# A gradient kernel: the first store of each trio on a second queue, ahead of the end of the last load

## Chip, core, metric

One core of one Trainium2 chip. The metric is the device time of the kernel in microseconds, median of several executions.

## The reference

```python
x = np.random.randn(8192, 8192).astype(np.float32)
def reference(x):
    return np.gradient(x, axis=1)
```

Along each row, an inner element becomes half the difference of its right and left neighbours; the two row ends become plain differences. Input and output are 268.4 MB each.

## The kernel before

32 tiles, each 128 partitions x two rows of 8192 floats (8.39 MB), go through three slots in SBUF. For each tile: a load, a tiny subtraction on GpSimd that puts the row ends aside (POOL in the profile), one pass on VectorE (DVE) that halves the differences, in place and shifted by 64 columns, a tiny copy that places the row ends, and a store. All transfers go through the sync engine's queue, in runs of three loads and three stores.

```python
R, NB, SH = 2, 3, 64                       # rows a tile, slots, shift
def load(i):
    b = slots[i % NB]
    ins = nc.sync.dma_start(out=b[:, SH : SH + W], in_=x_sets[i])
    loads.append(chain(i, ins, *([stores[i - NB]] if i >= NB else [])))   # waits for the slot's store

for i in range(NB): load(i)
for i in range(nsets):
    ins = nc.gpsimd.tensor_sub(out=ends[:, i], ...)           # row ends put aside
    at = [chain(i, ins, loads[i])]
    last = i == nsets - 1
    nr = 1 if last else R                                     # the last tile goes in two rows
    for r in range(0, R, nr):
        ins = nc.vector._custom_dve(...)                      # 0.5 * (right - left)
        halved = chain(i, ins, *at)
        placer = nc.gpsimd if i % 5 in (1, 3) and not last else nc.vector
        ins = placer.tensor_copy(...)                         # row ends placed
        placed = chain(i, ins, halved)
        ins = nc.sync.dma_start(out=out_sets[i, ...], in_=b[...])
        stores[i] = chain(i, ins, placed)
        at = [halved]
    if i % NB == NB - 1:                                      # three loads after three stores
        for k in range(i + 1, min(i + 1 + NB, nsets)): load(k)
```

## Time and profile before

| | before |
|---|---|
| time, median of the first 3 executions | 1248.08 us (1247.47 to 1248.88) |
| span of the profiled execution | 1245.0 us |
| moved | 536.88 MB, 431 GB/s over the span |
| VectorE busy | 45% |
| share of the 16 DMA engines' span taken by packets | 99.8% |

A page of the profile has, among others, the busy time of each engine, a row of 40 slices of the span (the busy share of the DMA engines in tenths, and GB/s), the DMA queues with their packets, and groups of instructions (line, engine, operation, shapes, count, busy us, mean ns, idle time before them and its cause). Two groups of before; after the first bar stand the busy time (us) and the mean duration (ns), after the second the idle time (us) and what ended it:

```profile
L81 DVE CUSTOM_DVE_ANT_0 slot<-slot 128x16382 f32<-128x16382 f32 (+1 forms) x33 | 551.3, 16706 | 667.9 <-POOL ends L70 667.9
L92 DVE COPY slot<-ends 128x4 f32<-128x4 f32 (+1 forms) x21 | 3.6, 172 | 0.7
```

VectorE has 667.9 us of idle time: nothing that it is spared can shorten the kernel by itself.

Below the page lie the trace's records of single DMA packets (start, duration, bytes, queue). No view prints them, so where I use them I give sums. They name neither the engine nor the direction: packets are joined end to start into 16 chains, one for each engine, and the order in which the transfers were issued tells loads from stores. Counts of matched packets are therefore good to a few per cent only. The landings on single engines are the trace's semaphore updates, 16 for each transfer; no view prints these either. A "long packet" is one of 65,536 bytes that took over 2.47 us instead of 2.418. The "packet excess" is the time of all packets above 2.418 us (1.21 for halves), from 5 us into the span on, divided by 16: what a mean engine lost. Before: 3.10 us.

### The profile page before, as it was taken

How to read it: one execution, taken by the hardware profiler on the slowest of the kernel's cores; microseconds unless marked ns; L12 is line 12 of the kernel's file. 1: busy time of each engine (PE TensorE's matmuls, PEld its weight loads, DVE VectorE, ACT ScalarE, POOL GpSimd, SP SyncE). 2: the span in 40 equal slices, each digit the busy share in tenths (PEclk: the TensorE clock that was granted, in tenths of full speed). 3: DMA queues.
4: the chain of work that ended last, by engine and by line, in shares of the span. 5: the costliest groups of instructions: out<-in, count | busy, mean ns of one | idle time of the engine just before them, and what ended most of it. 6: DMA issues, size and time to landing. Idle time of an engine off the chain costs nothing.

```text
span 1245.0 us, 241 instructions
## 1 busy us (share of the span) xinstructions
DVE 554.8 (45%) x54; POOL 8.8 (1%) x48
## 2 busy tenths in 40 slices
DVE  2850483079009603850582079009603840591083
POOL 0000000000000000000000000000000000000000
DMA  9999999999999999999999999999999999999999
GB/s 404 438 436 419 425 438 438 438 438 438 434 427 421 436 438 438 436 438 432 432 419 438 436 438 432 436 434 432 423 436 436 436 438 436 430 427 430 436 411 404
DMA packets 9361, 536.88 MB, mean 431 GB/s; under 512 B 1040, under 2 KB 1040, under 8 KB 1040
## 3 DMA queue, kind: packets, MB, share of 16 engines
q1 hardware_dynamic: 9360, 536.88, 99.8%
q14 instruction: 1, 0.01, 0.0%
HBM read 268.44 MB, written 268.44 MB: 431 GB/s over the span
## 4 chain that ended last, share of the span: by engine, by line
another core or an unknown queue 74%; DVE 18%; DMA 3%; issue 2%; POOL 1%; SPq 0%; POOLq 0%
DVE slot L81 18%; DMA slot<-in_x_dram 3%; POOL ends L70 0%; POOL slot L92 0%; SPq L60 0%; DVE slot L92 0%; POOLq L127 0%
## 5 line engine op out<-in xcount | busy, mean ns | idle before, releaser
L81 DVE CUSTOM_DVE_ANT_0 slot<-slot 128x16382 f32<-128x16382 f32 (+1 forms) x33 | 551.3, 16706 | 667.9 <-POOL ends L70 667.9
L70 POOL TENSOR_TENSOR ends<-slot 128x4 f32<-128x4 f32 x32 | 6.3, 198 | 988.8 <-DMA slot<-in_x_dram 988.8
L92 DVE COPY slot<-ends 128x4 f32<-128x4 f32 (+1 forms) x21 | 3.6, 172 | 0.7
L92 POOL COPY slot<-ends 128x4 f32<-128x4 f32 x12 | 2.3, 190 | 207.9 <-DVE slot L81 207.9
L116 POOL MEMSET const-bfloat16-1.0<- 128x1 bf16 x1 | 0.1, 102 | 0.0
L116 POOL MEMSET const-uint8-127<- 128x1 uint8 x1 | 0.1, 102 | 0.0
L116 POOL MEMSET const-float32-0.0<- 128x1 f32 x1 | 0.1, 99 | 0.2 <-issue 0.2
L116 POOL MEMSET const-float32-1.0<- 128x1 f32 x1 | 0.1, 99 | 0.0
## 6 DMA issues: line engine op xcount, KB each, us to landing
out_dram<-slot SPq DMA_DIRECT2D x2, 4096.0 KB, 20.2
slot<-in_x_dram SPq DMA_DIRECT2D x32, 58.0
out_dram<-slot SPq DMA_DIRECT2D x31, 40.3
```

Source lines behind the costliest of these rows:

```text
L70: ins = nc.gpsimd.tensor_sub(out=ends[:, i, :, :], in0=xin[:, :, 1 : m : m - 2], in1=xin[:, :, 0 : m - 1 : m - 2],)
L81: ins = nc.vector._custom_dve(dve_ops.TENSOR_TENSOR_REDUCE_SUB_MAX, out=b[:, c0:c1], in0=b[:, SH + c0 + 1 : SH + c1 + 1], in1=b[:, SH + c0 ...
L92: ins = placer.tensor_copy(out=res[:, :, 0 : m : m - 1], in_=ends[:, i, r : r + nr, :])
L116: nc = _bacc.Bacc("TRN2", target_bir_lowering=False, num_devices=1)
```

## The change

The intent: don't let the first store of a trio wait in the queue behind the last load. It goes on the ACT (ScalarE) queue and is let go when the first row of the middle tile is halved, so the engines have stores at hand before the loads are through. The middle tile's pass is cut in two rows to give that moment; ScalarE and GpSimd place the row ends. At the end, tile 29 counts as a "first": its store is held back behind loads 30 and 31.

```diff
+    next_loads = {i: range(i + 1, i + 1 + NB) for i in range(NB - 1, n3 - NB, NB)}
+    next_loads[n3 - 2] = range(n3, nsets)              # n3 = 30: loads 30, 31 after tile 28
+    firsts = [*range(0, n3, NB), n3 - 1]
     ...
-            nr = 1 if last else R
-            ...
-                placer = nc.gpsimd if i % 5 in (1, 3) and not last else nc.vector
-            ...
-            if i % NB == NB - 1:
-                for k in range(i + 1, min(i + 1 + NB, nsets)):
-                    load(k)
+            if i - 1 in firsts and i not in firsts or last:
+                at = halve(i, 0, 1, at)
+                if last:
+                    store(nc.sync, i, 0, 1, place(nc.vector, i, 0, 1, at))
+                else:
+                    store(nc.scalar, i - 1, 0, R, placed, at)      # the first store, gated
+                at = halve(i, 1, 1, at)
+            else:
+                at = halve(i, 0, R, at)
+            if last:
+                store(nc.sync, i, 1, 1, place(nc.vector, i, 1, 1, at))
+            else:
+                placed = place(nc.gpsimd if i % 4 == 1 else nc.scalar, i, 0, R, at)
+                if i not in firsts:
+                    store(nc.sync, i, 0, R, placed)
+            for k in next_loads.get(i, ()):
+                load(k)
```

(The helpers `store`, `halve`, `place` and `put_aside` hold the same calls as before.)

More of the change, by code (lines that the diff above doesn't have):

```diff
@@ L4 @@
 import concourse.tile as tile
-from concourse import bass_utils, dve_ops
+from concourse import bass_utils, dve_ops, mybir
 from concourse._compat import with_exitstack
@@ L41 @@
     ends = pool.tile([P, nsets, R, 2], f32, name="ends", tag="ends")
+    landed = mybir.DependencyInfo(mybir.DependencyClass.Sync, mybir.DependencyReason.DATA)
     loads, stores = [], [None] * nsets
@@ L61, in load, with store, put_aside, halve @@
         loads.append(chain(i, ins, *([stores[i - NB]] if i >= NB else [])))
+    n3 = (nsets - 2) // NB * NB
+    assert nsets - 2 == n3
+    next_loads = {i: range(i + 1, i + 1 + NB) for i in range(NB - 1, n3 - NB, NB)}
+    next_loads[n3 - 2] = range(n3, nsets)
+    def store(queue, i, r, nr, *needed):
+        ins = queue.dma_start(
+            out=out_sets[i, :, r * m : (r + nr) * m], in_=slots[i % NB][:, r * m : (r + nr) * m]
+        )
+        stores[i] = chain(i, ins, needed[0])
+        for o in needed[1:]:
+            tc.add_manual_dep(ins.ins, o.ins.name, landed, reason="before the end of the last load")
+    def put_aside(i):
+        xin = slots[i % NB][:, SH : SH + W].rearrange("p (t m) -> p t m", m=m)
+        ins = nc.gpsimd.tensor_sub(
+            out=ends[:, i, :, :],
+            in0=xin[:, :, 1 : m : m - 2],
+            in1=xin[:, :, 0 : m - 1 : m - 2],
+        )
+        return chain(i, ins, loads[i])
+    def halve(i, r, nr, at):
+        b = slots[i % NB]
+        c0, c1 = r * m + 1, (r + nr) * m - 1
+        ins = nc.vector._custom_dve(
+            dve_ops.TENSOR_TENSOR_REDUCE_SUB_MAX,
+            out=b[:, c0:c1],
+            in0=b[:, SH + c0 + 1 : SH + c1 + 1],
+            in1=b[:, SH + c0 - 1 : SH + c1 - 1],
+            s0=0.0,
+            s1=0.5,
+        )
+        return chain(i, ins, at)
+    def place(engine, i, r, nr, at):
+        res = slots[i % NB][:, r * m : (r + nr) * m].rearrange("p (t m) -> p t m", m=m)
+        to, of = res[:, :, 0 : m : m - 1], ends[:, i, r : r + nr, :]
+        ins = nc.scalar.copy(out=to, in_=of) if engine is nc.scalar else engine.tensor_copy(out=to, in_=of)
+        return chain(i, ins, at)
+    firsts = [*range(0, n3, NB), n3 - 1]
     with tc.manual_schedule():
@@ L66 @@
         for i in range(nsets):
-            b = slots[i % NB]
-            xin = b[:, SH : SH + W].rearrange("p (t m) -> p t m", m=m)
-            ins = nc.gpsimd.tensor_sub(
-                out=ends[:, i, :, :],
-                in0=xin[:, :, 1 : m : m - 2],
-                in1=xin[:, :, 0 : m - 1 : m - 2],
-            )
-            at = [chain(i, ins, loads[i])]
-            last = i == nsets - 1
-            nr = 1 if last else R
-            for r in range(0, R, nr):
-                c0, c1 = r * m + 1, (r + nr) * m - 1
-                ins = nc.vector._custom_dve(
-                    dve_ops.TENSOR_TENSOR_REDUCE_SUB_MAX,
-                    out=b[:, c0:c1],
-                    in0=b[:, SH + c0 + 1 : SH + c1 + 1],
-                    in1=b[:, SH + c0 - 1 : SH + c1 - 1],
-                    s0=0.0,
-                    s1=0.5,
-                )
-                halved = chain(i, ins, *at)
-                res = b[:, r * m : (r + nr) * m].rearrange("p (t m) -> p t m", m=m)
-                placer = nc.gpsimd if i % 5 in (1, 3) and not last else nc.vector
-                ins = placer.tensor_copy(out=res[:, :, 0 : m : m - 1], in_=ends[:, i, r : r + nr, :])
-                placed = chain(i, ins, halved)
-                ins = nc.sync.dma_start(
-                    out=out_sets[i, :, r * m : (r + nr) * m], in_=b[:, r * m : (r + nr) * m]
-                )
-                stores[i] = chain(i, ins, placed)
-                at = [halved]
@@ L99 @@
-            if i % NB == NB - 1:
-                for k in range(i + 1, min(i + 1 + NB, nsets)):
-                    load(k)
+            at = put_aside(i)
+            last = i == nsets - 1
+            if i - 1 in firsts and i not in firsts or last:
[7 more added lines that the diff above has]
+                at = halve(i, 0, R, at)
```

## The prediction

> **What bounds the kernel now.** I read the page first, then who waited for whom, then the GpSimd and queue rows in order of time, and last the trace's records of single DMA packets. The page:
>
> ```profile
> span 1245.0 us, 241 instructions
> DVE 554.8 (45%) x54; POOL 8.8 (1%) x48
> ...
> DMA  9999999999999999999999999999999999999999
> ...
> q1 hardware_dynamic: 9360, 536.88, 99.8%
> ...
> HBM read 268.44 MB, written 268.44 MB: 431 GB/s over the span
> ```
>
> The reader is to see that one queue keeps the 16 DMA engines busy 99.8% of the span, while VectorE, the only busy engine, works 45% of it. The array is read once and written once, so the bytes can't shrink. In the packet records nearly every packet of 65,536 bytes takes 2.418 us on its engine: 16 x 65,536 / 2.418 us = 433.7 GB/s. 536.88 MB at that rate are 1238.0 us. The first packet starts at 1.75 us and the last bytes are confirmed at 1244.1 us, so of the 1245.0 us of the profile 1238 are plain transfer, 1.75 start, about 1 end, and only some 4 us are spread over the middle. Everything that the change can win lies in those 4 us.
>
> Where do they lie? Each GpSimd subtraction starts 0.07 us after a load has landed, so its rows in order of time are a clock of the landings (start, duration, instruction, and in brackets the idle time before it). Two trios of loads and the last two loads:
>
> ```profile
> 22.70 0.20 POOL L70 TENSOR_TENSOR ends<-slot 128x4 f32<-128x4 f32 x1 [22.26 <-DMA slot<-in_x_dram]
> 42.04 0.20 POOL L70 TENSOR_TENSOR ends<-slot 128x4 f32<-128x4 f32 x1 [19.14 <-DMA slot<-in_x_dram]
> ...
> 62.45 0.20 POOL L70 TENSOR_TENSOR ends<-slot 128x4 f32<-128x4 f32 x1 [2.71 <-DMA slot<-in_x_dram]
> ...
> 721.14 0.20 POOL L70 TENSOR_TENSOR ends<-slot 128x4 f32<-128x4 f32 x1 [77.06 <-DMA slot<-in_x_dram]
> ...
> 740.49 0.20 POOL L70 TENSOR_TENSOR ends<-slot 128x4 f32<-128x4 f32 x1 [1.64 <-DMA slot<-in_x_dram]
> 760.50 0.20 POOL L70 TENSOR_TENSOR ends<-slot 128x4 f32<-128x4 f32 x1 [19.81 <-DMA slot<-in_x_dram]
> ...
> 1186.19 0.20 POOL L70 TENSOR_TENSOR ends<-slot 128x4 f32<-128x4 f32 x1 [77.05 <-DMA slot<-in_x_dram]
> 1205.53 0.20 POOL L70 TENSOR_TENSOR ends<-slot 128x4 f32<-128x4 f32 x1 [19.14 <-DMA slot<-in_x_dram]
> ```
>
> A tile of 8.39 MB takes 8 x 2.418 = 19.34 us. The second load of a trio lands 19.34 us after the first (42.04 - 22.70), but the third comes 20.41 us after the second in the first trio and 20.01 us in the one at 760. Over all ten trios the third load is late by 1.06, 0.01, 0.01, 0.04, 0.50, 0.61, 0.66, 0.17, 0.27 and 0.00 us: 3.3 us in all. The stretches from a third load to the next first load (three stores and a load) are four tiles long, 77.25 to 77.40 us against 77.38, and give 0.6 us of it back. So the slowest engine loses about 2.8 us in the kernel, all at the switch from loads to stores; the other switch, from stores to loads, is free. The packet records say the same: it is the last load packet of each engine before the first store that is long (3.2 to 3.5 us at 58 us, 2.6 to 3.2 at 639), averaged over the engines 0.24 us a switch.
>
> The last view is the queue's own waits and the end of the timeline:
>
> ```profile
> SPq L94 <- DVE slot L92: 525.7, 21, 55.9
> SPq L60 <- DMA out_dram<-slot: 373.2, 29, 19.2
> ```
> ```profile
> 1203.68 0.17 DVE L92 COPY slot<-ends 128x4 f32<-128x4 f32 x1
> 1203.88 19.93 SPq L94 DMA_DIRECT2D out_dram<-slot  x3
> ```
>
> These long waits are of the issuing sequencer, with up to three transfers queued ahead, and cost nothing: a store issued at 157.57 us runs only when the third load is through at 178.5. The one exception is the end. The store of tile 30 is issued at 1203.88 us, when the load of tile 31 ends on the 16 engines between 1202.9 and 1205.5 us. The early engines idle about 1.5 us on average, but the slowest has no gap: its next store lands at 1224.8, one tile after 1205.46. That hole evens out the engines' skew rather than costing the end.
>
> **What the Trainium skill says.** "DMA: Bandwidth & Descriptors", section "Where 436 GB/s comes from", puts the ceiling of the 16 ports at 435.2 GB/s; the trace agrees, 433.7 in the packets. The same page, "Issuing engines are not separate DMA queues", says that DMAs of the scalar and sync engines end up on the same 16 engines and interleave: no bandwidth is to be had from the second queue. Its section "Queues, rings and completion order" says that each engine takes turns between the queue rows that have work, a packet at a time; the trace of before uses one queue and can't show it, and my estimate below takes equal turns. "ScalarE: Activation LUTs", section "What ACT_TABLE_LOAD costs", measures 1283 ns for the load that ScalarE will need once; there is no ScalarE work in this trace to compare.
>
> **The change part by part.**
>
> 1. *Placing row ends.* 19 whole-tile VectorE copies of 172 ns (3.3 us) and some GpSimd ones go, and ScalarE does most of the placing. VectorE idles 667.9 us, so this is worth 0 on the path. A ScalarE copy of four elements might take 0.3 us instead of 0.17; it delays a store's issue by 0.1 us, with many us of queue ahead. The table load comes while the first load runs (22 us). 0 us.
>
> 2. *Row-wise middle tile.* One pass of 17.22 us becomes two of 8.69 and 8.60 as in the last tile of before: +0.1 us on an engine at 45%. 0 us.
>
> 3. *First store on the other queue.* Take the round whose loads land at 139.8, 159.1 and 178.5. The first row of the middle tile is done at 159.4 + 8.7 = 168.1 us. The store goes out then and starts about 1 us later (the first load was issued at 0.74 and moved at 1.75). Now the third load has 9.3 us left, and with equal turns ends at 169.2 + 18.6 = 187.8 instead of 178.5. The first store has by then done half; it shares the engines with the middle store and ends at 187.8 + 2 x 10.0 = 208. The third tile's pass ends at 188 + 17.4 = 205.5, and its store is queued at 206. Loads and two stores together fill the engines until 120.5 + 5 x 19.34 = 217.2 us, so the third store is there 11 us before it is needed. The next load waits for the first store (208), long before the queue reaches it at 236.5; the two after it wait for stores at 217 and 236.5, in time too. No new hole: the bytes still set the time, 0 us from scheduling.
>
> 4. *What the overlap does to the switch.* This is the disputed part. At best the engine has packets of both kinds in hand and the long last load packet goes away: -2.8 us on the slowest engine. At worst each load packet followed by a store packet pays the 0.24 us: 9.3 / 2.418, nearly 4 switches per engine and round instead of 1, so 3 x 0.24 x 10 = +7 us.
>
> 5. *The end.* Tile 29 is held back: loads 30 and 31 are now queued after the store of 28, and the store of 29 runs beside load 31. It fills the hole at 1203, and the last tile still goes out in two halves with nothing after it. The 1.5 us is the mean engine's, none of it the slowest's; I count 0, or some tenths if skew no longer builds up.
>
> Sum: -2.8 at best, +7 at worst. I weigh the good case somewhat higher, because the switch within one ordered queue is what seems to hold the last load packet up: about -1 us.
>
> **The rivals.** (a) *The switch vanishes*: 1248.1 - 2.8 = 1245.3 us. For it: two queues let an engine fetch from both sides; the loss stands only where a load meets a store in one queue. (b) *Mixing costs*: every alternation pays, 1248.1 + 7 = 1255 us. For it: the loss is seen on each engine just where the two directions meet. Against it: in two of ten rounds it was 0.01 us or less with the same meeting. (c) *Unequal turns*: if the sync queue were served first, the first store would starve behind two others, the next load would wait for it, and about 2 us per round would be empty: +20 us, 1268. If the other queue came first, the third load would land 19.3 us late, at 198, and its store be issued at 216, just when the engines run dry at 217: about 1 us a round, 1258. (d) *Nothing changes* since the switch to mixed stores only moves: 1248.
>
> **Range and chances.** (a) or a part of it has about half of the weight, (d) a quarter, (b) a fifth, (c) a twentieth. That gives 1247.0 us with 1244.0 to 1255.0 for 8 in 10. A floor stands at about 1244, since the transfer alone takes 1238.0 us, so over 2% faster (1223) is all but excluded: 0.01. Over 2% slower (1273) needs (c) or worse: 0.02. Within 2%: 0.97.
>
> **What would show it.** Right: DMA still 9 in all 40 slices; two queues, the new one with 10 to 11 stores (92 MB of 536.88); third loads landing 27 to 29 us after the second instead of 19.4 to 20.4; packet times of 2.418 us (or twice that where two overlap) with no long load packets at the switch; ScalarE under 10 us busy. If (b), dips in the GB/s row at every overlap and longer periods between the first loads of trios than 116.1 to 116.7 us. If (c), the sync queue's waits on stores end after the engines ran dry, and a slice falls below 9. The prediction is wrong if the packet rate itself differs when reads and writes of the HBM are mixed for about 19 us in each round, in either direction.

## The result, and the profile after

| | before | after |
|---|---|---|
| median | 1248.21 us (6 runs) | 1248.91 us (6 runs) |
| range | 1247.16 to 1248.94 | 1248.20 to 1249.84 |
| packet excess, profiled execution | 3.10 us | 5.63 us |
| last store landed on the first / the last of the 16 engines | 1243.9 / 1244.1 us | 1244.2 / 1246.8 us |

The ratio is 1.0006, with a 95% interval of 0.9993 to 1.0019. A ratio is the mean time of one kernel's fast runs over that of the other's fast runs of the same rounds, so not quite the ratio of the medians. Executions over 1.5% slower than the fastest of the same kernel are left out of the means. Unaltered in a later set of runs (b0 below) the changed kernel stood at 1.0017 (1.0005 to 1.0029). The profiled execution of after happened to be the slowest of its six.

The page of after, the rows that answer to those shown of before:

```profile
span 1247.8 us, 258 instructions
DVE 553.3 (44%) x46; ACT 5.8 (0%) x24; POOL 8.1 (1%) x44
...
DMA  9999999999999999999999999999999999999998
...
q1 hardware_dynamic: 7776, 444.60, 82.7%
q10 hardware_dynamic: 1584, 92.28, 17.1%
...
L110 ACT COPY slot<-ends 128x4 f32<-128x4 f32 x23 | 4.5, 197 | 1180.3 <-DVE slot L97 1180.3
...
L110 ACT ACT_TABLE_LOAD x1 | 1.3, 1283 | 0.7 <-PEq L151 0.7
```

The second queue, q10, carries 11 stores (92.28 MB); the two queues add up to the same 99.8%. ScalarE is busy 5.8 us. The engines are as full as before, so the scheduling left no hole; only the last slice has an 8.

Who waited on the sync queue, after:

```profile
SPq L76 <- ACT slot L110: 616.5, 15, 56.3
SPq L65 <- DMA out_dram<-slot: 326.6, 29, 33.8
```

As before these are waits of the sequencer with transfers queued ahead of it. They cost nothing as long as the DMA row stays full.

The second round of after in order of time (start, duration, engine, instruction; "x2" merges two issues, the second one 0.34 us before the end of the stretch):

```profile
140.10 0.20 POOL L86 TENSOR_TENSOR ends<-slot 128x4 f32<-128x4 f32 x1 [69.91 <-DMA slot<-in_x_dram]
...
159.45 0.20 POOL L86 TENSOR_TENSOR ends<-slot 128x4 f32<-128x4 f32 x1 [19.16 <-DMA slot<-in_x_dram]
...
168.45 0.34 ACTq L76 DMA_DIRECT2D out_dram<-slot  x1
...
177.35 27.60 SPq L76 DMA_DIRECT2D out_dram<-slot  x2
186.87 0.20 POOL L86 TENSOR_TENSOR ends<-slot 128x4 f32<-128x4 f32 x1 [27.23 <-DMA slot<-in_x_dram]
...
210.97 26.94 SPq L65 DMA_DIRECT2D slot<-in_x_dram  x3
```

And the same three landings in before:

```profile
139.84 0.20 POOL L70 TENSOR_TENSOR ends<-slot 128x4 f32<-128x4 f32 x1 [77.19 <-DMA slot<-in_x_dram]
159.18 0.20 POOL L70 TENSOR_TENSOR ends<-slot 128x4 f32<-128x4 f32 x1 [1.64 <-DMA slot<-in_x_dram]
178.54 0.20 POOL L70 TENSOR_TENSOR ends<-slot 128x4 f32<-128x4 f32 x1 [19.16 <-DMA slot<-in_x_dram]
```

The POOL rows are the landings. The third load lands 27.4 us after the second (19.4 in before), because from 173 us on it shares the engines with the first store. The first store is issued at 168.45 us and has landed by 210.95, where the next load is issued. The third store is issued at 177.35 + 27.60 - 0.34 = 204.6 us; the middle one landed on the slowest engine at 218.2. So the queue had some 12 us in hand.

Inside the overlap the packet records alternate: after one packet of q10 on an engine comes one of q1, then one of q10, each 2.418 to 2.427 us long. That is the equal turn that was assumed. (Once a round, where the sync queue passes from the third load to the middle store, q10 has two turns in a row.) The long packets haven't gone away. They stand once per round at the place where the first store comes in: at 53.2 us, where the packet of the third load just ahead of the first store packet took 3.4 to 3.9 us on all 16 engines, and so on near 170, 288, 404, 520 us. 182 of them are load packets directly ahead of a q10 packet. An engine goes from a load packet to a store packet about three times in an overlap, and of the three it is nearly always the first that is long. Before, they stood at 58.2 us and at the ends of the third loads.

### The profile page after: what moved, and what is told of

It is laid out like the page before. It is cut to its first block, busy times and chain, and to the rows that moved or that the text cites. A ratio compares the mean times of both kernels' runs of the same rounds, so it can differ in the third digit from the quotient of the medians.

```text
span 1247.8 us, 258 instructions
## 1 busy us (share of the span) xinstructions
DVE 553.3 (44%) x46; ACT 5.8 (0%) x24; POOL 8.1 (1%) x44
## 3 DMA queue, kind: packets, MB, share of 16 engines
q10 hardware_dynamic: 1584, 92.28, 17.1%
## 4 chain that ended last, share of the span: by engine, by line
DMA 72%; DVE 11%; another core or an unknown queue 11%; issue 2%; POOL 0%; SPq 0%; POOLq 0%; ACTq 0%
DMA slot<-in_x_dram 38%; DMA out_dram<-slot 35%; DVE slot L97 11%; POOL ends L86 0%; SPq L65 0%; POOL slot L110 0%; DVE slot L110 0%; POOLq L162 0%; ACTq L76 0%
## 5 line engine op out<-in xcount | busy, mean ns | idle before, releaser
L97 DVE CUSTOM_DVE_ANT_0 slot<-slot 128x8190 f32<-128x8190 f32 (+1 forms) x44 | 553.0, 12569 | 660.7 <-POOL ends L86 660.3
L110 ACT COPY slot<-ends 128x4 f32<-128x4 f32 x23 | 4.5, 197 | 1180.3 <-DVE slot L97 1180.3
L110 ACT ACT_TABLE_LOAD x1 | 1.3, 1283 | 0.7 <-PEq L151 0.7
```

The lines of the kernel that those rows point to most:

```text
L97: ins = nc.vector._custom_dve(dve_ops.TENSOR_TENSOR_REDUCE_SUB_MAX, out=b[:, c0:c1], in0=b[:, SH + c0 + 1 : SH + c1 + 1], in1=b[:, SH + c0 ...
L110: ins = nc.scalar.copy(out=to, in_=of) if engine is nc.scalar else engine.tensor_copy(out=to, in_=of)
```

## The experiments

All kernels below gave correct results. Twelve were run; each was timed against the kernel before in the same rounds.

### a1: the side work alone

```diff
 # after, with every store on the sync queue in the old order
-                else:
-                    store(nc.scalar, i - 1, 0, R, placed, at)
-                if i not in firsts:
-                    store(nc.sync, i, 0, R, placed)
+                store(nc.sync, i, 0, R, placed)
 # and the loads after each third tile, as before
```

> Only the side work of the change: ScalarE places row ends, the middle tile goes by rows, but every store stays on the sync queue in the old order with the old end. Theory 1 (the time is set by packets and the long load packet before a round's first store): same as before within 0.1% (ratio 0.999 to 1.001), two-engine page with one queue, and long packets at the ends of the third loads as before, about 2.4 us in all as a mean over the engines. Theory 3 (the side work costs something that hid a gain of the queue): 0.1 to 0.3% slower than before, with a store issued later than the queue needs it. It also shows whether the pattern of the ten switches (0.96 us in the first, none in the second and tenth) repeats or is chance.

Measured: 1247.78 against 1247.49 us, ratio 1.0001 (0.9988 to 1.0014). The side work costs nothing. Its page has one queue and the same ScalarE group as after:

```profile
q1 hardware_dynamic: 9360, 536.88, 99.8%
...
L109 ACT COPY slot<-ends 128x4 f32<-128x4 f32 x23 | 4.5, 198 | 1198.0 <-DVE slot L96 1198.0
```

The long packets at the ten switches from loads to stores, as means of the engines, were 1.19, 0.28, 0.03, 0.21, 0.05, 0.51, 0.18, 0.09, 0.05 and 0.67 us here, and 0.96, 0.00, 0.10, 0.07, 0.20, 0.41, 0.17, 0.12, 0.37 and 0.00 us in before. So about 1 us at the first switch repeats, and the pattern of the others is chance. In all, 3.64 us of packet excess against 3.10.

### a2: the held-back store alone

```diff
 # before
-            if i % NB == NB - 1:
-                for k in range(i + 1, min(i + 1 + NB, nsets)):
-                    load(k)
+            if i == nsets - 4:
+                load(nsets - 2)
+                load(nsets - 1)
+            elif i % NB == NB - 1 and i + NB < nsets:
+                for k in range(i + 1, i + 1 + NB):
+                    load(k)
```

> Only the held-back store: before, with loads 30 and 31 put ahead of the store of tile 29, all on the sync queue. The hole of 1.5 us (mean of the engines) at 1203 us is filled. Theory 1 says that the hole cost the slowest engine nothing: same time within 0.1%, and the last landings of the 16 engines then lie 2 to 3 us apart instead of 0.2 us. If the hole did cost, it is 1 to 1.5 us faster (ratio 0.999).

Measured: 1247.85 us, ratio 1.0002 (0.9990 to 1.0014). The hole at 1203 us is gone, and nothing is won. The last store landed on the first engine at 1241.5 us and on the last at 1244.2; in before it was 1243.9 and 1244.1. The hole was a pause of the engines that were ahead, in which they waited for the slowest; without it they end early and the slowest ends at the same moment.

### a3: the overlap made permanent

```diff
 # before
-                ins = nc.sync.dma_start(out=out_sets...      # store
+                ins = nc.scalar.dma_start(out=out_sets...
-            if i % NB == NB - 1:
-                for k in range(i + 1, min(i + 1 + NB, nsets)):
-                    load(k)
+            if i + NB < nsets:
+                load(i + NB)
```

> The overlap made permanent: all loads on the sync queue, each store on the other as soon as it is placed, so packets of both kinds alternate nearly all the time. Theory 1 (paid once when stores begin after a run of loads, alternation free): one long packet per engine near 41 us and hardly any after it; the time is 1238 plus start and end, and perhaps 1 to 2 us of hole in front of the last tile: 1243 to 1247 us, ratio 0.996 to 0.999. Theory 2 (each meeting of a load and a following store costs 0.24 us on the mean engine, or mixed traffic is slower by itself): 256 meetings per engine, up to 60 us, so 1260 to 1310.

Measured: median 1250.44 us, but between 1246.31 and 1263.67 over six runs; ratio 1.0043 (1.0007 to 1.0080). GB/s in the 40 slices, of an execution at 1258.57 us:

```profile
GB/s 403 432 434 434 432 434 432 434 434 434 434 434 434 434 434 434 434 434 434 434 432 436 432 434 434 432 432 434 434 432 434 434 434 434 432 430 436 407 403 275
```

From the second slice to the 37th the engines carry 430 to 436 GB/s, about the rate of pure loads or pure stores (433.7). Loads and stores take turns there for 1100 us: of 4096 load packets, 2873 could be matched with a store packet right behind them, and 86 of these were long, 3%. The packet excess is 4.40 us, of which 0.78 at one place, 43.5 us, where the first store comes in. This refutes the second theory, that each meeting costs: it asked for up to 60 us.

Why is it not faster, then? The loads' landings, late in the same execution:

```profile
1144.08 0.20 POOL L70 TENSOR_TENSOR ends<-slot 128x4 f32<-128x4 f32 x1 [21.49 <-DMA slot<-in_x_dram]
...
1183.04 0.20 POOL L70 TENSOR_TENSOR ends<-slot 128x4 f32<-128x4 f32 x1 [38.76 <-DMA slot<-in_x_dram]
...
1221.81 0.20 POOL L70 TENSOR_TENSOR ends<-slot 128x4 f32<-128x4 f32 x1 [38.57 <-DMA slot<-in_x_dram]
```

The last load landed at 1221.7 us on the slowest engine. On the first one it landed at 1203.7, 18 us earlier. Early in the span the same distance was below 5 us. One engine collected long packets one by one (0.1 to 1.3 us each, from about 630 us on), and GpSimd started only when the last of the 16 was through (1221.81 us). Then the last tile's pass and its stores began late, and the slices at the end fall to 407, 403 and 275.

### a4: one store, one load in turn, on one queue

```diff
 # before
-            if i % NB == NB - 1:
-                for k in range(i + 1, min(i + 1 + NB, nsets)):
-                    load(k)
+            if 1 <= i and i + 2 < nsets:
+                load(i + 2)
```

> One queue, but after the start one store and one load in turn instead of three and three: 30 switches from loads to stores instead of 10. Theory 1 with a fixed price per beginning of stores (0.24 us mean over the engines): 20 more, +5 us, ratio 1.004. If the price grows with the run of loads before it (8 packets instead of 24), less: +0 to +2 us. Theory 2 gives +5 us as well, but then a3_two_queues must be slow.

Measured: 1249.77 us, ratio 1.0016 (1.0004 to 1.0028). Three times as many switches cost 2 us, not 5. The mean engine's packet excess is 3.87 us, of which 1.00 at the first switch, so that the 29 others cost about 0.1 us each, against 0.24 in before with the first one counted (0.16 without). A fixed price of 0.24 us per switch is refuted: 20 more switches cost the mean engine 0.8 us, not 5. That it is the shorter run of loads (8 packets instead of 24) that lowers the price fits, but is not shown by itself. The slowest engine tells the time here too: the last store landed between 1240.8 us on the first engine and 1246.8 on the last.

### b0: the changed kernel once more

No edit.

> The changed kernel once more, unaltered, as the measure for the others of this set. Theory 1 (the price is paid once per round, by the load packets that stand directly before the first store packets; turns after that are free): 1.000 to 1.001 of before; long load packets in front of the other queue's packets, 0.4 to 0.5 us a round as a mean over the engines, as in the first profile (5.2 us in all).

Measured: 1250.05 us against 1248.25, ratio 1.0017 (1.0005 to 1.0029). The long packets stand where they stood, but are fewer: 115 load packets ahead of the other queue's packets, out of 1215 that could be matched; 4.10 us of packet excess instead of 5.63. The last store landed between 1242.4 us on the first engine and 1246.4 on the last. So in this execution the mean engine lost 1 us more to long packets than in before, and the slowest ended about 2 us later.

### b1: a late gate

```diff
 # after
-                else:
-                    store(nc.scalar, i - 1, 0, R, placed, at)
                 at = halve(i, 1, 1, at)
+                if not last:
+                    store(nc.scalar, i - 1, 0, R, placed, at)
```

> The first store waits for both rows of the middle tile, so it is issued near 177.3 us instead of 168.4 in the second round and starts when the third load ends: same queue, no overlap. If the larger price of the changed kernel (5.2 us of long packets against 2.1 to 2.9 with one queue) comes from starting stores in the middle of a load, it falls back to 2 to 3 us and the time to 0.999 to 1.000 of before. If it comes from the second queue by itself, it stays near 5 us.

Measured: 1255.17 us, ratio 1.0059 (1.0047 to 1.0071). That was expected by none. The first store was issued at 177.73 us in the second round and the third load landed at 179.3, so there was hardly an overlap, and the price at the beginning of the stores did fall in nine of ten rounds, to between 0.04 and 0.25 us on the mean engine. But a new price came up at the other switch. GB/s in the 40 slices of its page (31 us each):

```profile
GB/s 404 433 435 433 435 404 435 435 435 429 433 410 435 435 435 435 435 435 402 435 435 435 435 435 429 429 414 435 435 435 435 429 412 431 435 435 429 431 412 402
```

A slice counts the packets that start in it: 13 starts an engine give 435, one fewer gives 402. So the row shows that the engines were busy, but not at which switch the time went. The packet records do: the last store packets before the loads are long by 0.6 to 0.9 us on the mean engine (at 116, 234, 351 us and on, in nine of ten rounds), where before, a1 and a2 had 0.00 to 0.04 there. The packet excess is 10.5 us, 7.4 more than in before, which is the 7 us of the result. Why this switch, which is free with one queue and in the changed kernel, is not free here, the traces don't say.

### b2: no gate

```diff
 # after
-                else:
-                    store(nc.scalar, i - 1, 0, R, placed, at)
-                if i not in firsts:
-                    store(nc.sync, i, 0, R, placed)
+                store(nc.scalar if i in firsts else nc.sync, i, 0, R, placed)
```

> The first store goes out as soon as its tile is placed, so it overlaps the whole third load (some 19 us of it instead of 9). Theory 1: twice as many turns, yet the same long packets, once per round (about 5 us in all). The gate then matters only for the schedule: the third load lands near 197.8, its pass ends at 215.6 and its store reaches the engines near 217, just when they run dry, so up to 1 us of hole per round: 1248 to 1258 us. Theory 2 (each turn costs): long packets all over the overlap, about 10 us.

Measured: 1313.37 us, ratio 1.0513 (1.0492 to 1.0533): the hole that was expected, but several times as large. The row of the DMA engines, and the second round in order of time:

```profile
DMA  9999997999899999999998999999989989999978
```
```profile
176.92 46.20 SPq L76 DMA_DIRECT2D out_dram<-slot  x2
205.05 0.20 POOL L86 TENSOR_TENSOR ends<-slot 128x4 f32<-128x4 f32 x1 [45.83 <-DMA slot<-in_x_dram]
205.28 17.22 DVE L97 CUSTOM_DVE_ANT_0 slot<-slot 128x16382 f32<-128x16382 f32 x1 [28.61 <-POOL ends L86]
...
223.17 21.71 SPq L65 DMA_DIRECT2D slot<-in_x_dram  x3
```

And the same stretch of time in both kernels (start and end, its length, busy us and instructions of VectorE, ScalarE and GpSimd, clock, DMA share, GB/s), first without the gate, then the changed kernel:

```profile
214.00:224.00 10.00, 8.50 (x1) 0.00 (x0) 0.19 (x1) 1.00 0.31 131
```
```profile
214.00:224.00 10.00, 0.00 (x0) 0.00 (x0) 0.00 (x0) 1.00 1.13 492
```

The third load landed at 205.0 us instead of the 197.8 of the estimate, its pass ended at 222.5, its store was issued at 176.92 + 46.20 - 0.34 = 222.8, and the engines ran dry from 216 to 223.6. (A share over 1 is packets counted by their start.) In the profiled execution, 68.9 us longer than that of before, the mean engine idled some 42 us more (3 to 7 us in most rounds after the first, about 10 us near the end), and the long packets told of below cost 26.7 us more: that makes up the difference. The loads' landings say where the hole of 7 us came from: on the first engine the third load landed at 194.5, on the last at 205.0. In this round fifteen engines kept 2.418 us a packet; one, which had taken its first store packet while the others were still loading, had long packets of both kinds (3.42, 3.25, 2.63, 3.14 and 3.25 us among its first seven) and fell behind. In the first round the overlap was as cheap as expected (0.9 us lost on the mean engine, the third load landed at 79.1), and from the third round on long packets stood on many engines. In all, the packet excess is 29.8 us, where theory 1 expected about 5, and 286 of 1273 matched meetings of a load packet with a store packet were long. So theory 1 is not the whole of it either: the alternation can be free, as in a3, but isn't always. What the gate gives the changed kernel is the reserve: with it, the third store is issued 12 us before it is needed. It also halves the overlap, and no run separates the two.

### b3: the permanent overlap with a finer end

```diff
 # a3, the last tile in pieces of a quarter, a quarter and a half
-            nr = 1 if last else R
-            for r in range(0, R, nr):
-                c0, c1 = r * m + 1, (r + nr) * m - 1
+            h = m // 2
+            pieces = [(0, h), (h, m), (m, 2 * m)] if last else [(0, R * m)]
+            for p0, p1 in pieces:
+                c0 = p0 + (p0 % m == 0)
+                c1 = p1 - (p1 % m == 0)
```

(The placing and the store take the same bounds.)

> The permanent overlap of a3_two_queues with the last tile in pieces of a quarter, a quarter and a half, so that its first store is ready about 7 us after the last load instead of 11. Where all engines keep pace this saves the hole of about 2 us at the end: best executions 1244 to 1245 us. If an engine falls behind again as in a3_two_queues (20 us at the last load), the median stays at 1248 to 1252 and the spread between executions over 5 us.

Measured: median 1250.02 us, between 1245.66 and 1256.61; ratio 1.0019 (0.9996 to 1.0042). The best execution is 1.3 us below the fastest of before in that set (1246.94), and close to the floor that the prediction drew. But in the profiled execution (1251.43 us) the last store landed on the last engine 7 us after the first, and the times scatter over 11 us. It beats neither kernel.

### c1 to c4: engines put out of step on purpose

From b2 I formed a fourth theory: alternation is free only while all engines go in the same direction at the same time, and one out of step pays. To test it, a small extra transfer goes ahead of everything. With 8 rows it reaches 8 engines, with 16 rows all 16. It brings 32 KB rows of tile 1 that the proper load brings again, so the results stay right.

```diff
 # c1: a3; c2: a3 with 16 for 8; c3: after; c4: before
+        ins = nc.sync.dma_start(out=slots[1][0:8, SH : SH + m], in_=x_sets[1, 0:8, 0:m])
+        nudges.append(chain(1, ins))           # load 1 waits for it
```

> The permanent overlap of a3_two_queues, with one more transfer of 8 rows of 32 KB ahead of everything (rows that a later load brings again), which should reach 8 of the 16 engines and put them half a packet behind the other 8. Theory 4 (alternation is free only while all engines move in the same direction at the same time; an engine out of step with the others pays 0.2 to 1.0 us a packet, as the straggler of b2_no_gate did): far slower, 10 to 40%, or at least over 1270 us, with long packets of both kinds all over. Theory 1 alone: 1.2 us more than a3_two_queues, 1247 to 1252.

> The control: the same extra transfer with 16 rows, so that all 16 engines are put back by the same half packet and stay in step. Both theories: a3_two_queues plus 1.2 us, median 1247 to 1255, with hardly a long packet in the first half.

> The changed kernel with the 8-row transfer, half of its engines out of step by half a packet. Its overlap lasts about 18 us a round, 7 packets per engine. Theory 4: each of these pays, some 2 to 5 us a round, so 1265 to 1300 unless the engines find their step again. Theory 1: 1250 to 1252.

> The kernel before with the 8-row transfer. Directions meet only where the runs of three loads and three stores touch, so being out of step should cost little under both theories: 1248 to 1251 us. A difference from c3_after_8 of over 10 us would show that the overlap makes the kernel depend on the engines' step.

| | median, us | range, us | ratio to before | 95% interval |
|---|---|---|---|---|
| c1, permanent overlap, 8 rows | 1269.25 | 1257.34 to 1275.96 | 1.0189 | 1.0138 to 1.0239 |
| c2, permanent overlap, 16 rows (3 fast runs; a slow one took 1281.60) | 1261.13 | 1254.27 to 1264.98 | 1.0098 | 1.0058 to 1.0137 |
| c3, changed kernel, 8 rows | 1251.18 | 1250.25 to 1251.82 | 1.0025 | 1.0011 to 1.0040 |
| c4, before, 8 rows | 1249.90 | 1249.71 to 1250.22 | 1.0016 | 1.0001 to 1.0031 |

The one trace of c1 speaks against the theory, but it is of its fastest execution (1257.34 us). Two of the four took 1275 and 1276 us, over the 1270 that the theory asked for at least, and of these there is no trace. GB/s of the fastest:

```profile
GB/s 376 428 428 432 430 424 434 434 430 434 432 434 434 420 432 434 434 432 434 434 434 430 434 434 434 434 434 434 434 434 434 434 434 434 434 434 434 434 434 292
```

Its engines were out of step: near 300 us their packets began all over the 2.4 us of a packet, and some loaded while others stored. Still the slices read 434 from the 23rd on to the 39th, and 4.67 us of packet excess are hardly more than the 4.40 of a3. There were no long packets "all over": an engine out of step doesn't always pay. What this execution loses, it loses at the start and at the end. Why the others were slower stays open. c2, meant as the control, was nearly as slow and as scattered, so the two medians don't isolate anything either. c3 lies 1.3 us above c4, about what separates the changed kernel from before without the extra transfer (0.7 and 1.8 us): no dependence of 10 us on the step.

One thing in these traces points the other way round. In c3 and c4 the first switch from loads to stores, which cost the mean engine 0.96 to 1.32 us in before, after, a1, a2, a4 and b0, cost 0.01 and 0.00 us. Near 46 us, before that switch, the engines' packets began within 0.6 us of each other in before and after, but over some 2.3 us in c3 and c4. So the price near 1 us was not there with the engines out of step. That is one profile of each kernel, and whether it was the step or the extra transfer itself, no run tells apart.

## Why the prediction was right, point by point

**What bounds it.** Right. The bytes set the time in both kernels; no run beat the floor of about 1244 us, and the best execution of all was 1245.66. It is this that put the time within the forecast. The range of 1244 to 1255 us held rivals (a), (b) and (d) alike, so that 1248.91 fell into it says nothing for (a), which was favoured and failed: in that part the forecast was saved by the width of its range.

**Steps 1 and 2, the side work.** Right, by a1 (1.0001). The table load took 1283 ns as cited. A ScalarE copy took 197 ns, less than the 0.3 us allowed for; two row passes took 17.41 us instead of 17.22.

**Step 3, the schedule.** Right, within 3 us everywhere:

| second round, us | predicted | measured |
|---|---|---|
| first row of the middle tile done, first store issued | 168.1 | 168.45 |
| third load landed | 187.8 | 186.8 |
| third store issued | 206 | 204.6 |
| first store landed | 208 | 210.95 |
| the engines would run dry | 217.2 | 218.2 (middle store landed) |

One part was off: the first store was to start about 1 us after its issue, which was read from an empty queue. With full engines its first packet began at 172.9 us, 4.4 us after the issue. So it shared less of the third load's time than predicted: the load landed 1 us earlier, and the store 3 us later.

**Step 4, the switch.** This is the step whose term was mis-sized, and as far as the runs tell it had the wrong sign: +0.7 us with an interval that includes no change, and +1.8 us clear of it in b0. The sum put it at about -1 us between -2.8 and +7. Neither end came true. Rival (a), that the long packets vanish, is refuted: with a second queue they stand at the moment at which the first store comes in, one cluster a round. Rival (b), that each alternation costs 0.24 us, is refuted as a rule by a3: 3% of the matched meetings were long, over 1100 us. In the changed kernel 182 load packets were long out of 1232 turns from q1 to q10, but over half of these turns were from one store to another; of those from a load to a store some 40% were long (181 of 448), nearly all where the first store comes in. What holds is rival (d) with a small surcharge: the loss at the beginning of the stores only moves into the third load, and grew. The packet excess was 5.63 and 4.10 us in two profiles of the changed kernel against 3.10, 3.64 and 3.03 us in three profiles with one queue and three and three. That is 0.5 to 2.6 us more for the mean engine. (With the 8-row transfer it was 3.43 in c3 against 2.33 in c4.) This doesn't set the time directly: filling the hole at the end gives the mean engine 1.5 us back, and in b0 the last landings of the 16 engines lay at 1243.5 us in the mean, earlier than in the kernel before (1244.0). It is the slowest engine that ended later: at 1246.8 and 1246.4 us, against 1244.1 in before and 1244.2 in a2, which fills the same hole with one queue. A late gate (b1) lowers the price at this switch and meets a larger one at the other.

**Step 5, the end.** Right: a2 fills the same hole alone and wins nothing (1.0002), because the hole belonged to the engines that were ahead.

**Rival (c), unequal turns.** Didn't come: the queues took strict turns. But b2 shows that a hole of the kind that it described is real when the reserve is gone: 7 us in the second round, from one engine that fell behind.

**Slips in the working.** They change nothing above. The loss of the slowest engine, 3.3 less 0.6 us, is 2.7 and not 2.8. By the list of landings three of ten third loads, not two, were late by 0.01 us or less. The first loads of trios came 116.0 to 116.7 us apart, but the first two 117.1. And the weights given to the rivals make a mean of about 1248.8 us (0.5 x 1245.3 + 0.25 x 1248 + 0.2 x 1255 + 0.05 x 1263, the middle of the two times given for (c)), not 1247.0.

**What stays open.** Why a load packet is long when the first store comes in after a run of loads, why that price is near 1 us at the first switch of most profiled executions (not of b1, c3 and c4) and scattered after it, why one engine falls behind in some executions, why the longer overlap of b2 was dear from its third round on when the permanent one of a3 was cheap, and why b1 pays at the other switch. Alternation by itself (a3) and being out of step by itself (the fastest execution of c1) are not enough to cause it.

## What to carry to other kernels

When the DMA engines are full, first work out what is left above bytes over packet rate: here 4 us of 1245, so no rearrangement of queues could have been worth 2%. A second queue brings no bandwidth, and it delays the load that it overlaps; what that load feeds then needs a reserve. If a second queue is used at all, a gate like the one here gives it (the same kernel without the gate: +5.1%, of which the holes were the larger part and long packets the rest); here the single queue was at least as fast. Judge small losses by the slowest of the 16 engines: a pause of the engines that are ahead is not a loss, and long packets that fall on a single engine are.

## What the Trainium skill lacked or had wrong

- "DMA: Bandwidth & Descriptors", "Queues, rings and completion order", says that an engine drains a packet of some 9 to 17 descriptors before it turns to the next queue row. The runs agree with turns: for these transfers, with 65,536 contiguous bytes a partition, the turn is one recorded packet of 65,536 bytes (2.418 us), and q1 and q10 alternate. How many descriptors such a packet holds, the trace doesn't say.
- The same page has nothing on the loss when stores begin after a run of loads: 0.0 to 1.3 us per switch for the mean engine here, about 1 us at the first one in most profiles, about 0.1 us after runs of 8 packets (a4).
- No page says how far the 16 engines drift apart under a load that keeps them full: the last load's landings lay 2.6 us apart in before (1202.9 to 1205.5 us, evened out by the hole that follows) and 18 us in a3; the last store's 2.6 and 4.0 us in two executions of the changed kernel and 6.1 in a4.
- The same page, "Issuing engines are not separate DMA queues", says that a second issuing engine only saves issue time. For bandwidth the runs agree (434 GB/s in a3). It lacks the other side: the second queue moves the landings of the first one's transfers (27.4 us instead of 19.4 for a load), and without a reserve, and with the longer overlap, the kernel was 5.1% slower (b2).
